# Moving operands at other byte offsets, and eight loads and three fills issued by GpSimd, in a one-core decoder layer

## The chip, the core and the metric

The kernel runs on one core of a Trainium2 chip. The metric is the device time of one launch in microseconds, the median of several runs. The engines have short names here: PE is TensorE (its matmuls), PEld its loads of the stationary operand, DVE is VectorE, ACT is ScalarE, POOL is GpSimd, and SP is the engine whose queue issues most transfers. Each engine takes its instructions in the order in which they were built.

## What is computed

One layer of a decoder, for 256 tokens of width 2048, in float32. It has three parts, each followed by a layer norm over `ALPHA * h + f(h)`:

```python
mix = hybrid_mixer(h, w_in, w_out, ...)     # S5 state space | stick-breaking heads | NSA heads, then w_out
xa = memory_cross_attention(h, mem, wq, wkv, wo)
ff = conv_ffn(h, w_up, conv_w, conv_b, w_down)   # 2048 -> 11264, conv, gated gelu, 5632 -> 2048
```

In the NSA attention the logits of every head get a bias that depends on the distance of query and key, `rel_bias[t5_bucket(dist)]`. The kernel holds that bias in the tile `slab`, with 16 heads of 256 columns each for every partition.

## The kernel before

**Products in three passes.** Every weight is read from memory as float32 in chunks of 128 x 1024 (`raw`, four buffers, issued by SP). ACT copies a chunk rounded into `hi`, DVE subtracts and writes the rest into `lo` (lines 291 and 292, three buffers of each). Activations are stored in two such parts as well. A product is then three matmuls: hi with hi, hi with the activations' rest, lo with hi. PE needs two operands for each: a stationary one of 128 columns, which a weight load brings in, and a moving one that streams through.

**Which operand moves.** Where the result is wanted as features by tokens (`mm3`, lines 306 to 308: all input projections but the values, the up-projection), the weights are stationary and 256 columns of activations move. Where it is wanted as tokens by columns (`mm3x`, lines 314 to 316: value projections, `w_out`, `wo`, `w_down`), the activations are stationary and `hi` and `lo` move, 512, 304 or 256 columns at a time. The residual's 2048 columns are done as three blocks of 512 and two of 256 (`RES_COLS`). One 128-row slice of the inner dimension gives six such matmuls a column block, three for each half of the tokens. So `w_out` (16 slices) has 288 matmuls of 512 columns and 192 of 256. `w_down` has 44 slices, the first 16 of which are in the tile `A` and the others in the tile `act`: 288 of 512 columns with `A` and 504 with `act`. Its last 256 columns are done last, and four of their chunks are held in the tiles `mix0` to `mix3`, which move in place of `hi` and `lo` there.

**Where the tiles lie.** Each pool follows the one before it in SBUF, and `gap` puts unused bytes between some. From the built program's addresses, counted modulo 256 bytes: all `hi` and `lo` buffers begin at 32, `A` and `mix0` to `mix3` at 224, `act` and `ox` (the cross-attention's output) at 32, `mixk` at 32. All slices of them that a matmul reads step by multiples of 512 bytes, but for those of 304 columns. So the distance from the stationary operand's start to the moving one's, modulo 256, is 192 in nearly all of `mm3`, 64 in `mm3x` where `A` or a `mix` tile is stationary, and 0 where `act` or `ox` is.

**The end of the mixer.** Four things stand here in a row on PE, and the same order is kept in both kernels: the keys (`nsa_keys`, 24 matmuls for each chunk of weights, results in three banks `pj`), the gate of the S5 group (`s5_out`, tile `s5zs`, four groups of 12 matmuls), the first three query projections (48 matmuls each), and then the NSA attention's first scores (lines 1011 and 1012, into `mx`), which need the queries' second part `nq` from DVE (line 971). Later queries and `w_out` run between the pieces of the attention. The gate goes gelu (line 765, ACT), table load, split into `s5zs`, matmuls, exp (line 782, ACT), reciprocal and product (lines 786 and 787, DVE), split into `mix0`.

`slab` shares its space with the tile `Es` of the S5 scan, so its eight loads of 256 KB (line 962) may start once the scan's last output matmuls have read `Es`. They were written for ACT's queue, and ACT issues them there before it goes on:

```python
        with self.lane("first"):
            for c in range(n):
                src = bass.AP(g_dr.tensor, g_dr.offset + 127 - c, ...)
                self.nc.scalar.dma_start(self.slab[c:128:n], src)
```

A scheduler orders each engine's instructions when the kernel is built, by priorities of lanes and its own model of times. It is run anew for a changed kernel.

Of the kernel before, what the change touches and what calls it, by code (L numbers as in the profile page):

```python
# [9 lines left out]
F32R = mybir.dt.float32r  # L10
# [15 lines left out]
BIG = 1e30  # L26
# [8 lines left out]
RES_COLS = ((0, 512), (512, 512), (1024, 512), (1536, 256), (1792, 256))  # L35
CST_AT = 3
SKEW = 16
NORM0, NORM1, HOLD = 3, (2,), 2
TABLE_PACE, SCAN_PACE = 0.8, 2.8
BUCKET_FROM = [16, 21, 27, 35, 46, 59, 77, 99, 128, 166, 216]  # L40
# [157 lines left out]
class Program:  # L198
# [24 lines left out]
        self.pq = pool("pq", 1, space=bass.MemoryType.PSUM)  # L223
        self.dram = pool("dram", 1, space=bass.MemoryType.DRAM)

    def gap(self, name, size):

        self.ctx.enter_context(self.tc.tile_pool(name=f"gap_{name}", bufs=1)).tile(
            [128, size // 4], F32, name=f"gap_{name}")

    @contextmanager
# [31 lines left out]
        return self.pq.tile([128, 512], F32, name="pb")  # L263


    def weights(self, src, n=1024, into=None):
        nc = self.nc
        with self.lane("split"):
            raw = self.wraw.tile([128, 1024], F32, name="raw")
            self.last_load = nc.sync.dma_start(raw[:, :n], src)  # L270
            parts = self.split_chunk(raw, n, into)
        self.mm_marks = self.mm_marks[1:] + [self.last_mm]
        self.credit += self.pace
        while self.credit >= 1:
            self.credit -= 1
            self.step()
        return parts
# [2 lines left out]

        return self.background is not None and next(self.background, None) is not None

    def split_chunk(self, raw, n, into=None):
        nc = self.nc
        with self.lane("split"):
            if into is not None:
                hi, lo = into
            else:
                hi = self.whi.tile([128, 1024], F32R, name="hi")
                lo = self.wlo.tile([128, 1024], F32R, name="lo")  # L290
            self.last_hi = nc.scalar.copy(hi[:, :n], raw[:, :n])  # L291
            self.last_lo = nc.vector.tensor_sub(lo[:, :n], raw[:, :n], hi[:, :n].bitcast(F32))  # L292
            hold = self.holds.pop(0) if self.holds else None
            if hold is not None:
                self.after(self.last_lo, hold)
        return hi, lo
# [38 lines left out]
    def to_cols(self, w, X, cols, kk, k0, k1):  # L335

        ps = [self.pj.tile([128, 512], F32, name="pj") for _ in range(2)]
        for c in range((k1 - k0) // kk):
            parts = self.weights(w[c], kk * cols)
            for tok in range(2):  # L340
                k = k0 + c * kk
                self.chunk_cols(ps[tok], parts, X, tok, cols, range(k, k + kk), k == k0,
                                k + kk == k1)
        return [p[:, :cols] for p in ps]
# [10 lines left out]
    def to_residual(self, w, X, k0, k1, scaled=True, final=True, load=None, late=0, keep=(),  # L355
                    between=None):

        first = 0  # L360
        if final:
            self.st = self.stat.tile([128, 2, len(RES_COLS), 6], F32, name="st")
        early = len(RES_COLS) - late
        for c0, n in RES_COLS[:early]:
            kk, cs = 1024 // n, slice(c0, c0 + n)
            if load is not None:
                with self.lane("split"):
                    self.after(self.nc.sync.dma_start(self.R[:, :, cs], load[:, :, cs]),
                               self.last_load)
            steps = (k1 - k0) // kk  # L370
            ps = self.to_cols(w[first:first + steps], X, n, kk, k0, k1)
            first += steps
            for tok in range(2):
                self.add(ps[tok], tok, c0, n, scaled, final)
        if not late:
            return
        chunks = []
        for g, (c0, n) in enumerate(RES_COLS[early:]):
            kk = 1024 // n
            for k in range(k0, k1, kk):  # L380
                chunks.append((g, c0, n, range(k, k + kk), w[first]))
                first += 1
        held, beside = {}, None
        turning = min(3, len(chunks) - len(keep))
        fixed = range(len(keep))
        order = list(range(len(chunks)))
        for tok in range(2):
            left = [(k1 - k0) * n // 1024 for _, n in RES_COLS[early:]]
            ps = {}
            for i in order:  # L390
                g, c0, n, ks, src = chunks[i]
                if i not in held:
                    held[i] = self.weights(src, into=keep[i] if i in fixed else None)
                new = g not in ps
                if new:
                    ps[g] = self.pj.tile([128, 512], F32, name="pj")
                left[g] -= 1
                self.chunk_cols(ps[g], held[i], X, tok, n, ks, new, left[g] == 0)
                if left[g] == 0:
                    self.add(ps[g][:, :n], tok, c0, n, scaled, final)  # L400
                    if beside is not None:
                        next(beside, None)
            if tok == 0:
                beside = between()
                next(beside, None)
                again = order[len(keep):-turning]
                for i in again:
                    del held[i]
                if again:
                    order = order[-turning:] + list(fixed) + again  # L410
# [540 lines left out]
    def nsa_slab(self):  # L951


        g_dr, n = self.g_dr, 128 // SKEW

        self.nq = self.nsp.tile([128, 8, 2, 256], F32R, name="nq")
        self.slab = self.slabp.tile([128, NH, 256], F32, name="slab", tag="Es")
        with self.lane("first"):
            for c in range(n):
                src = bass.AP(g_dr.tensor, g_dr.offset + 127 - c,  # L960
                              [[384 - n, SKEW], [SKEW * 384, NH], [1, 256]])
                self.nc.scalar.dma_start(self.slab[c:128:n], src)

    def nsa_queries(self):
        a, V, S, q = self.a, self.nc.vector, self.nc.scalar, self.nq
# [8 lines left out]
    def nsa(self):  # L974
        nc, a, V, S = self.nc, self.a, self.nc.vector, self.nc.scalar
# [10 lines left out]


        pc = p.tile([128, 2, NH, 32], F32, name="pc")
        V.memset(pc, 0.0)
        tcs = [p.tile([128, 2, 4, NC_], F32, name=f"tcs{i}") for i in range(2)]  # L990
        for t in tcs:
            V.memset(t[:, 0], BIG)
        halves = lambda t: t.rearrange("p (c k) -> p c k", c=2)
        for quad in range(4):
            o = self.pq.tile([128, 2, 256], F32, name="pa")
            start = [None, None]
            for b in range(2):
                n = 128 if b else 128 + NK
                for gl in range(2):
# [3 lines left out]
                    for r in range(2):  # L1003
                        h = h0 + r
                        kh, kl = (k[:, h // 8, gl].rearrange("p c n -> p (c n)") for k in ks[b])
                        t = qcol(h)
# [198 lines left out]
    def cross_attention(self, H):  # L1205
        nc, a, V, S = self.nc, self.a, self.nc.vector, self.nc.scalar
        mm = nc.tensor.matmul
        scale = 128.0 ** -0.5
        with ExitStack() as st:
            p = st.enter_context(self.tc.tile_pool(name="xap", bufs=1))  # L1210
            w = st.enter_context(self.tc.tile_pool(name="xaw", bufs=2))
            ox = p.tile([128, 4, 2, 256], F32R, name="ox")
# [59 lines left out]

    def ffn(self, H):
        nc, a, V, S = self.nc, self.a, self.nc.vector, self.nc.scalar
        self.gap("f", 128)
        p = self.ctx.enter_context(self.tc.tile_pool(name="ffp", bufs=1))
        w = self.ctx.enter_context(self.tc.tile_pool(name="ffw", bufs=2))
        cv = p.tile([128, NFF, 2, 4], F32, name="cv")
# [5 lines left out]
        for i in range(NFF):  # L1284
            c = []
# [50 lines left out]
```

## Time and profile before

| | us |
|---|---|
| median of 3 runs (1293.86 to 1295.22) | 1294.0 |
| the profiled execution's own time | 1293.79 |
| its span | 1292.0 |
| PE busy | 1254.6 (97%) |
| DVE busy | 883.8 (68%) |
| ACT busy | 659.9 (51%) |
| POOL busy | 13.3 (1%) |

A matmul's own duration in the profile holds the time that it takes to run through the array, and matmuls overlap. What one costs in a full stream is the distance from its start to the next one's. A stretch in which PE does one kind of work without a break therefore gives the pace: its length over the number of matmuls that the program has there.

### The profile page before, as it was taken

To read this page: it belongs to the slowest core of one execution; us is meant where nothing else is said; L and a number is where in the kernel's file an instruction comes from. 1 tells how busy PE (TensorE), PEld (TensorE's weight loads), DVE (VectorE), ACT (ScalarE), POOL (GpSimd) and SP (SyncE) were. 2 spreads that over 40 slices of the span, in tenths; PEclk is the share of its full clock that TensorE was granted. 3 is DMA by queue.
4 is the path that set the end of the run, shared out by engine and by line. 5 is a ranking of instruction groups with operands and counts; after the bars stand their busy time and mean duration, and the time that the engine had idled before them with its cause. 6 is when DMAs were issued, how large, how long until landed. Compare 5 with 4: busy or idle time off the path is not lost.

```text
span 1292.0 us, 23010 instructions
## 1 busy us (share of the span) xinstructions
PE 1254.6 (97%) x9222; PEld 1160.8 (90%) x9222; DVE 883.8 (68%) x1510; ACT 659.9 (51%) x1032; POOL 13.3 (1%) x23
## 2 busy tenths in 40 slices
PE   7999999999999999899999999999999999999996
PEld 7788898988779899799999999999999988888896
DVE  7799896877765675776666666666666654544557
ACT  6884434666554355455555555555555543334342
POOL 0200000000000000000000000000000000000000
PEclk9999999999999999999999999999999999999998
DMA  8653348633447564445555565565655755656573
GB/s 306 192 167 128 99 137 224 186 117 103 131 168 279 189 208 151 137 142 194 192 192 195 196 195 191 191 193 194 196 196 190 254 193 195 195 184 199 187 228 130
DMA packets 68886, 237.37 MB, mean 184 GB/s; under 512 B 7787, under 2 KB 10652, under 8 KB 68012
## 3 DMA queue, kind: packets, MB, share of 16 engines
q1 hardware_dynamic: 64720, 230.21, 53.7%
q10 hardware_dynamic: 3276, 3.47, 1.2%
q0 software_dynamic: 784, 2.23, 0.9%
q8 instruction: 72, 1.18, 0.4%
q14 instruction: 34, 0.28, 0.1%
HBM read 231.82 MB, written 2.49 MB: 181 GB/s over the span
## 4 chain that ended last, share of the span: by engine, by line
PE 76%; DVE 3%; ACT 1%; issue 1%; DMA 0%; DVEq 0%; ACTq 0%
PE pj L306 14%; PE pj L307 14%; PE pj L308 14%; PE pj L314 9%; PE pj L316 9%; PE pj L315 9%; PE pa L1048 2%; DVE lo L292 1%; PE mx L1011 1%; PE mx L1012 1%; DVE R L1144 1%; DVE R L1149 1%; PE op L1041 0%; PE pb L1041 0%; ACT hi L291 0%
## 5 line engine op out<-in xcount | busy, mean ns | idle before, releaser
L292 DVE TENSOR_TENSOR lo<-raw,hi 128x1024 fp32r<-128x1024 f32 (+2 forms) x403 | 488.5, 1212 | 339.0 <-ACT hi L291 337.9
L291 ACT CAST hi<-raw 128x1024 fp32r<-128x1024 f32 (+2 forms) x403 | 419.8, 1042 | 510.7 <-PE pj L307 276.4
L307 PE MATMUL pj<-mix,hi 128*128 128x256 f32 x1380 | 381.9, 277 | 0.0
L306 PE MATMUL pj<-mix,hi 128*128 128x256 f32 x1380 | 381.1, 277 | 0.0
L308 PE MATMUL pj<-mix,lo 128*128 128x256 f32 x1380 | 381.0, 276 | 0.0
L307 PEld LDWEIGHTS pj<-mix,hi 128*128 128x128 f32 x1380 | 259.2, 188 | 0.1
L308 PEld LDWEIGHTS pj<-mix,lo 128*128 128x128 f32 x1380 | 259.2, 188 | 0.1
L306 PEld LDWEIGHTS pj<-mix,hi 128*128 128x128 f32 x1380 | 259.1, 188 | 0.2
L306 PE MATMUL pj<-A,hi 128*128 128x256 f32 x496 | 141.2, 288 | 8.6 <-ACT hi L291 8.6
L308 PE MATMUL pj<-A,lo 128*128 128x256 f32 x496 | 139.2, 288 | 4.2 <-DVE lo L292 4.0
L307 PE MATMUL pj<-A,hi 128*128 128x256 f32 x496 | 140.4, 286 | 0.0
L306 PEld LDWEIGHTS pj<-A,hi 128*128 128x128 f32 x496 | 95.9, 194 | 11.2 <-ACT hi L291 9.3
L308 PEld LDWEIGHTS pj<-A,lo 128*128 128x128 f32 x496 | 94.6, 194 | 8.1 <-DVE lo L292 5.6
L307 PEld LDWEIGHTS pj<-A,hi 128*128 128x128 f32 x496 | 96.1, 194 | 1.9 <-issue 1.9
L315 PE MATMUL pj<-lo,act 128*128 128x512 f32 (+1 forms) x280 | 96.8, 347 | 0.0
L316 PE MATMUL pj<-hi,act 128*128 128x512 f32 (+1 forms) x280 | 96.8, 347 | 0.0
L315 PE MATMUL pj<-lo,A 128*128 128x512 f32 (+2 forms) x288 | 96.3, 336 | 0.0
L316 PE MATMUL pj<-hi,A 128*128 128x512 f32 (+2 forms) x288 | 95.6, 333 | 0.0
L314 PE MATMUL pj<-hi,A 128*128 128x512 f32 (+2 forms) x288 | 91.0, 334 | 0.0
L314 PE MATMUL pj<-hi,act 128*128 128x512 f32 (+1 forms) x280 | 89.7, 347 | 0.0
L315 PEld LDWEIGHTS pj<-lo,A 128*128 128x128 f32 x288 | 54.1, 188 | 6.5 <-issue 1.1
L315 PEld LDWEIGHTS pj<-lo,act 128*128 128x128 f32 x280 | 52.9, 189 | 6.6
(324 smaller groups left out, 1809.5 us busy)
## 6 DMA issues: line engine op xcount, KB each, us to landing
raw<-in_w_up SPq DMA_DIRECT2D x176, 512.0 KB, 4.2
raw<-in_w_down SPq DMA_DIRECT2D x92, 512.0 KB, 3.3
raw<-in_win_c SPq DMA_DIRECT2D x48, 512.0 KB, 3.9
raw<-in_w_out SPq DMA_DIRECT2D x32, 512.0 KB, 4.0
raw<-in_win_sv SPq DMA_DIRECT2D x8, 512.0 KB, 4.7
raw<-in_wk_m SPq DMA_DIRECT2D x8, 512.0 KB, 4.9
raw<-in_wv_m SPq DMA_DIRECT2D x8, 512.0 KB, 4.2
raw<-in_wq SPq DMA_DIRECT2D x8, 512.0 KB, 4.1
```

What stands on the lines that cost most here:

```text
L291: self.last_hi = nc.scalar.copy(hi[:, :n], raw[:, :n])
L292: self.last_lo = nc.vector.tensor_sub(lo[:, :n], raw[:, :n], hi[:, :n].bitcast(F32))
L306: mm(ps, hi, ah, start=start, stop=False)
L307: mm(ps, hi, al, start=False, stop=False)
L308: self.last_mm = mm(ps, lo, ah, start=False, stop=stop)
L314: mm(ps, ah, hi, start=start, stop=False)
L315: mm(ps, ah, lo, start=False, stop=False)
L316: self.last_mm = mm(ps, al, hi, start=False, stop=stop)
L1011: mm(zs, q[:, t, gl, qs], kh[:, 0:m], start=True, stop=False)
L1012: mm(zs, q[:, t, gl, qs], kl[:, 0:m], start=False, stop=True)
L1048: ins = mm(o[64 * r:64 * r + 64, gl, 128 * c:256], vv[:, c, v, :], pt[:, k0:k1], start=start[r] is None, stop=False, skip_group_check=True)
L1144: ins = V.scalar_tensor_tensor(r, r, mean, self.gb[:, 0, c0:c1], ALU.subtract, ALU.mult)
```

## The change

`hi` and `lo` buffers become 1088 columns wide in place of 1024, so each takes 4352 bytes, 17 times 256. Chunks for `mm3x` are written from column 48 on (192 bytes) where the column block is 512 wide, and from column 32 on (128 bytes) where it is 256. Those for 304 columns, for `mm3`, and the held chunks stay at column 0. A gap of 192 bytes ahead of the cross-attention's pool moves `ox`, and the gap ahead of the feed-forward's pool goes from 128 to 64 bytes, which moves `act`. In the built program `A`, `act`, `ox` and `mix0` to `mix3` now all begin at 224 modulo 256, `mixk` stays at 32, and the matmuls' distances change so:

| moving columns | stationary | matmuls | start of moving, stationary, distance before | after |
|---|---|---|---|---|
| 256 | `A`, `mix0` to `mix3` | 576 | 32, 224, 64 | 160, 224, 192 |
| 256 | `act`, `ox` | 384 | 32, 32, 0 | 160, 224, 192 |
| 512 | `A`, `mix0` to `mix3` | 672 | 32, 224, 64 | 224, 224, 0 |
| 512 | `act`, `ox` | 528 | 32, 32, 0 | 224, 224, 0 |
| 512 (held in `A`) | `ox` | 48 | 224, 32, 192 | 224, 224, 0 |

The loads of `slab` are issued by POOL, and three fills (`pc` and two `tcs`, tiles of the attention) go from DVE to POOL.

```diff
+MOVING_AT = {512: 48, 256: 32}
...
-                hi = self.whi.tile([128, 1024], F32R, name="hi")
-                lo = self.wlo.tile([128, 1024], F32R, name="lo")
+                hi = self.whi.tile([128, 1088], F32R, name="hi")
+                lo = self.wlo.tile([128, 1088], F32R, name="lo")
+                at = MOVING_AT.get(cols, 0)
+                hi, lo = hi[:, at:], lo[:, at:]
...
-            parts = self.weights(w[c], kk * cols)
+            parts = self.weights(w[c], kk * cols, cols=cols)
...
-                    held[i] = self.weights(src, into=keep[i] if i in fixed else None)
+                    held[i] = self.weights(src, into=keep[i] if i in fixed else None, cols=n)
...
-                self.nc.scalar.dma_start(self.slab[c:128:n], src)
+                self.nc.gpsimd.dma_start(self.slab[c:128:n], src)
...
-        V.memset(pc, 0.0)
+        nc.gpsimd.memset(pc, 0.0)
...
-            V.memset(t[:, 0], BIG)
+            nc.gpsimd.memset(t[:, 0], BIG)
...
+            self.gap("x", 192, st)
...
-        self.gap("f", 128)
+        self.gap("f", 64)
```

ACT's queue at the end of the S5 scan, before. `kh0` and `kh1` are parts of the keys, `s5u` is the scan's output, `hi_2616` and `hi_2646` are the weights of the last key projection and `hi_2682` those of the gate:

```order
L938 CAST kh0_2091<-pj_2401 64x2x128 x2
L962 DMA slab_2794<-g_dr_1514 16x16x256 x8
L291 CAST hi_2616<-raw_2614 128x1024
L291 CAST hi_2646<-raw_2644 128x1024
L938 CAST kh0_2091<-pj_2468 64x2x128 x2
L765 ACTIVATE s5u_198<-s5u_198 128x1024
L253 ACT_TABLE_LOAD
```

And now:

```order
L943 CAST kh0_2091<-pj_2401 64x2x128 x2
L770 ACTIVATE s5u_198<-s5u_198 128x1024
L254 ACT_TABLE_LOAD
L984 ACTIVATE gate_2116<-gate_2116 128x96
L296 CAST hi_2616<-raw_2614 128x1024
L943 CAST kh0_2091<-pj_2468 64x2x128 x2
L304 CAST s5zs_2538<-s5u_198 128x4x256
L296 CAST hi_2646<-raw_2644 128x1024
```

The eight loads are gone from this queue, and the gelu with its table load now stands ahead of the two splits.

DVE's queue at the first scores of the attention, before (`pj_2803` and `pj_2868` are the first two query projections, `mx_3334` the first scores):

```order
L292 TENSOR_TENSOR lo_3002<-raw_2999,hi_3001 128x1024
L989 MEMSET pc_3326 128x1024
L992 MEMSET tcs0_3328 128x60
L992 MEMSET tcs1_3329 128x60
L300 TENSOR_TENSOR mix0_2535<-s5z_2768,mix0_2535 128x256
L971 SCALAR_TENSOR_TENSOR nq_2793<-pj_2803,nq_2793 64x256
L971 SCALAR_TENSOR_TENSOR nq_2793<-pj_2868,nq_2793 64x256
L292 TENSOR_TENSOR lo_3032<-raw_3029,hi_3031 128x1024
L1015 ISA tt_3339,mn_3340<-mx_3334,slab_2794 128x128
```

And now:

```order
L297 TENSOR_TENSOR lo_3002<-raw_2999,hi_3001 128x1024
L305 TENSOR_TENSOR mix0_2535<-s5z_2768,mix0_2535 128x256
L976 SCALAR_TENSOR_TENSOR nq_2793<-pj_2803,nq_2793 64x256
L976 SCALAR_TENSOR_TENSOR nq_2793<-pj_2868,nq_2793 64x256
L297 TENSOR_TENSOR lo_3032<-raw_3029,hi_3031 128x1024
L976 SCALAR_TENSOR_TENSOR nq_2793<-pj_2803,nq_2793 64x256
L976 SCALAR_TENSOR_TENSOR nq_2793<-pj_2868,nq_2793 64x256
L1020 ISA tt_3339,mn_3340<-mx_3334,slab_2794 128x128
```

The fills have left, and the second pair of `nq` parts, which stood between two heads' softmax steps, now stands ahead of the first.

On POOL, whose last work before was the fill of `kl1`, the program now ends:

```order
L936 MEMSET kl1_2544 128x1024
L967 DMA slab_2794<-g_dr_1514 16x16x256 x8
L994 MEMSET pc_3326 128x1024
L997 MEMSET tcs0_3328 128x60
L997 MEMSET tcs1_3329 128x60
```

Nothing of POOL's stands behind these. PE's order is the same up to the first scores; within the attention the pieces of later queries and of `w_out` fall elsewhere among its steps, and from the memory's keys on it is the same again.

## Rows read from the trace of the kernel before

**Rows 1.** The chain that ended last, by engine (the page, part 4).

```profile
PE 76%; DVE 3%; ACT 1%; issue 1%; DMA 0%; DVEq 0%; ACTq 0%
```

**Rows 2.** Windows: stretch, length, busy of PE, PEld, DVE, ACT, POOL; clock; DMA.

```profile
390.94:412.71 21.77, 21.77 (x194) 21.77 (x193) 11.77 (x14) 8.45 (x8) 0.00 (x0) 1.00 0.87 313
1037.65:1059.63 21.98, 21.98 (x99) 18.04 (x97) 11.35 (x12) 10.77 (x12) 0.00 (x0) 1.00 0.58 192
1059.63:1097.73 38.10, 38.10 (x170) 31.54 (x168) 17.37 (x15) 14.70 (x14) 0.00 (x0) 1.00 0.58 193
1217.84:1229.14 11.30, 11.30 (x97) 11.30 (x96) 6.98 (x8) 4.20 (x4) 0.00 (x0) 1.00 0.55 173
1229.14:1249.29 20.15, 20.15 (x170) 20.15 (x169) 10.78 (x9) 9.56 (x10) 0.00 (x0) 1.00 0.67 211
1250.71:1255.03 4.32, 4.32 (x39) 4.32 (x38) 3.68 (x6) 2.10 (x2) 0.00 (x0) 1.00 0.88 262
535.82:541.43 5.61, 5.61 (x26) 4.50 (x25) 4.70 (x14) 0.41 (x2) 0.00 (x0) 1.00 0.01 3
```

**Rows 3.** ACT in order of time around the loads of `slab` (start, us; idle before, releaser).

```profile
214.40 9.10 ACTq L962 DMA_DIRECT2D slab<-g_dr  x8
223.59 1.99 ACT L291 CAST hi<-raw 128x1024 fp32r<-128x1024 f32 x2 [9.04 <-DMA slab<-g_dr]
226.38 1.06 ACT L765 ACTIVATE s5u<-s5u 128x1024 f32<-128x1024 f32 x1
227.45 1.28 ACT L253 ACT_TABLE_LOAD   x1
```

**Rows 4.** PE in order of time, from the keys to the first scores.

```profile
222.17 0.28 PE L308 MATMUL pj<-A,lo 128*128 128x256 f32 x1
224.69 0.39 PE L306 MATMUL pj<-A,hi 128*128 128x256 f32 x1 [2.24 <-ACT hi L291]
225.95 0.47 PE L308 MATMUL pj<-A,lo 128*128 128x256 f32 x1 [0.76 <-DVE lo L292]
...
237.24 0.39 PE L306 MATMUL pj<-s5zs,hi 128*128 128x256 f32 x1 [2.01 <-ACT s5z L782]
...
258.25 0.28 PE L308 MATMUL pj<-A,lo 128*128 128x256 f32 x1
...
262.48 0.36 PE L1011 MATMUL mx<-kh,nq 128*128 128x256 f32 x1 [2.98 <-DVE nq L971]
```

**Rows 5.** Windows of two stretches with a lower clock, columns as in rows 2.

```profile
226.10:229.50 3.40, 3.40 (x17) 3.40 (x18) 1.75 (x4) 3.35 (x5) 0.00 (x0) 0.50 1.12 206
263.60:267.10 3.50, 3.50 (x19) 3.50 (x18) 2.37 (x13) 0.99 (x4) 0.00 (x0) 0.51 0.16 67
```

**Rows 6.** DVE in order of time, from the stalled split to the first bias.

```profile
214.96 0.47 DVE L190 SCALAR_TENSOR_TENSOR s5u<-s5u,s5prm,pa 128x256 f32<-128x256 f32 x1
224.67 1.23 DVE L292 TENSOR_TENSOR lo<-raw,hi 128x1024 fp32r<-128x1024 f32 x1 [8.78 <-ACT hi L291]
...
237.55 1.76 DVE L786 RECIPROCAL s5z<-s5z 128x128 f32<-128x128 f32 x2
...
256.03 0.91 DVE L989 MEMSET pc<- 128x1024 f32 x1 [0.16 <-DVE lo L292]
256.90 0.18 DVE L992 MEMSET tcs<- 128x60 f32 x2
...
259.31 0.29 DVE L1015 CUSTOM_DVE_ANT_0 tt<-mx,slab 128x128 f32<-128x128 f32 x1
```

**Rows 7.** Transfers: issuing queue, count, KB each, median us from issue to landing.

```profile
slab<-g_dr ACTq DMA_DIRECT2D x8, 256.0 KB, 10.3
s5us<-Ec POOLq DMA_DIRECT2D x12, 128.0 KB, 5.3
```

**Rows 8.** POOL in order of time, its transfers of `s5us`.

```profile
35.40 5.04 POOL L496 DMA_DIRECT2D s5us<-Ec  x9 [31.98 <-ACT Ec L299]
41.31 1.76 POOL L496 DMA_DIRECT2D s5us<-Ec  x3 [0.87 <-DMA s5us<-Ec]
```

More of the change, by code (lines that the diff above doesn't have):

```diff
@@ L224, in __init__, with gap @@
         self.dram = pool("dram", 1, space=bass.MemoryType.DRAM)
-    def gap(self, name, size):
-        self.ctx.enter_context(self.tc.tile_pool(name=f"gap_{name}", bufs=1)).tile(
+    def gap(self, name, size, ctx=None):
+        (ctx or self.ctx).enter_context(self.tc.tile_pool(name=f"gap_{name}", bufs=1)).tile(
             [128, size // 4], F32, name=f"gap_{name}")
@@ L263, in turn, with weights @@
         return self.pq.tile([128, 512], F32, name="pb")
-    def weights(self, src, n=1024, into=None):
+    def weights(self, src, n=1024, into=None, cols=None):
         nc = self.nc
@@ L270, in weights @@
             self.last_load = nc.sync.dma_start(raw[:, :n], src)
-            parts = self.split_chunk(raw, n, into)
+            parts = self.split_chunk(raw, n, into, cols)
         self.mm_marks = self.mm_marks[1:] + [self.last_mm]
@@ L281, in step, with split_chunk @@
         return self.background is not None and next(self.background, None) is not None
-    def split_chunk(self, raw, n, into=None):
+    def split_chunk(self, raw, n, into=None, cols=None):
         nc = self.nc
```

## The prediction, made before the changed kernel was run

> **What bounds the kernel now.** I read the chain of waits first: PE has 76% of it and no other engine more than 3% [rows 1]. So time is won where a matmul gets cheaper or where PE stands still, and the change touches both. For the first I read windows in which PE does one kind of work without a break. For the second I read PE in order of time around the loads of `slab`, then ACT and DVE there, which PE waits for.
>
> **Pace and offset.** The reader is to divide a window's length by the matmuls that the program has in it (the count in the row also holds the few that only reach in over an edge). With 256 moving columns [rows 2]: distance 192 (row 1, the keys of the memory, 192 matmuls) 21.77 / 192 = 113.4 ns; distance 64 (row 4, `A` stationary, 96) 11.30 / 96 = 117.7 ns; distance 0 (row 5, `act` stationary, 168) 20.15 / 168 = 119.9 ns; distance 0 with both at 224 (row 6, held chunks with `A`, 36) 4.32 / 36 = 120.0 ns. With 512 columns: distance 64 (row 2, `A`, 96) 21.98 / 96 = 229.0 ns; distance 0 (row 3, `act`, 168) 38.10 / 168 = 226.8 ns; distance 192 (row 7, chunks held in `A` with `ox`, 24) 5.61 / 24 = 233.8 ns. Rows 2 to 5 lie behind one another in `w_down`, at full clock, with the same transfers and with DVE and ACT half idle, so what differs is the address. The two rows at distance 0 with 256 columns agree though one has its operands at 32 and the other at 224: that speaks for the distance and against the place. I therefore take the distance as what sets the pace: 192 is best for 256 columns, 0 is best for 512.
>
> The change puts every stream of 256 columns at distance 192 and every one of 512 at 0. Worked out by the counts of the table in the section on the change, all on PE's own stream, where nothing hides it:
> - 576 matmuls from 117.7 to 113.4: 576 x 4.3 = 2.5 us.
> - 384 from 119.9 to 113.4: 384 x 6.5 = 2.5 us.
> - 672 from 229.0 to 226.8: 672 x 2.2 = 1.5 us.
> - 48 from 233.8 to 226.8: 0.3 us; 528 stay at 226.8.
>
> Sum 6.8 us. No row shows moving operands at 160, nor 512 columns with both at 224. The bounds are therefore the best and the worst pace of that width in any row. For 256 columns the worst is 120.0, 576 x 2.3 = 1.3 us lost. For 512 it is 233.8, 672 x 4.8 + 528 x 7.0 = 6.9 us lost. So the term lies between -6.8 and +8.2 us. I take -6.8, since the distance explains all seven rows. `hi` and `lo` as stationary operands keep their 32 modulo 256, so the up-projection, at distance 192 already, costs what it did. The wider buffers and the offsets cost ACT and DVE nothing: they write as many columns. The gaps move only tiles that ACT and DVE use beside PE.
>
> The Trainium skill (SBUF — State Buffer, section "Who interferes with whom") gives PE two independent read ports, one for the moving operand and one for the weight load, and says that PE never waits on anyone. By that rule no offset could change a pace, and this term would be 0. The seven windows disagree with it, with 113.4 against 120.0 ns.
>
> **The loads of `slab` leave ACT.** Issuing eight loads keeps ACT from 214.40 to 223.5; the two splits behind them had been ready, as their 9.04 us of wait for nothing but these transfers say [rows 3]. DVE sits 8.78 us behind ACT [rows 6]. PE still has split weights until 222.17, then waits 2.24 us for `hi` and 0.76 us for `lo` [rows 4], and after these waits the granted clock falls to half for 3.40 us [rows 5], which costs half of that, 1.7 us. These three, 4.7 us, hang on ACT's queue directly and go with it: that is the lower bound.
>
> What ACT did late made more late: gelu and table load at 226.38 and 227.45 [rows 3], in the new order next after the scan's output at 215.43 [rows 6]. From there come PE's 2.01 us in the gate and the 2.98 us at the first scores, which wait for `nq` behind DVE's backlog [rows 4], and the second fall of the clock, again half of 3.50 us [rows 5]. These are 2.0 + 3.0 + 1.7 = 6.7 us more, so the upper bound is 11.4 us.
>
> To choose, I walk the new orders with the rows' durations. ACT: gelu 215.4 to 216.5, table load to 217.8, gate to 218.1, `hi_2616` to 219.1, with `lo` at 220.3; PE wants them at 222.3, no wait. `hi_2646` waits for its buffer until 219.5, comes behind two other pieces of ACT at 221.9, `lo` at 223.2; wanted at 225.0. The gate's weights are split at 224.9 and `s5zs` at 222.0; wanted at 227.8. The gate's second group finds its bank free. The third and fourth need the exp of the first and second, at 230.0 and 232.2, wanted at 230.7 and 232.1. The first query projection needs the last of the keys' parts out of its bank: behind a reciprocal pair of 1.76 us [rows 6] and a split that is 234.3, wanted at 233.7, so 0.6 us of waiting is left. Three projections of 48 at 113.4 ns bring PE to 250.7 in place of 258.4 [rows 4]. The last splits for them come at 246.4 (wanted at 248.0), the first `nq` at 249.6 (wanted 250.7), their second pair at 251.6, before PE, which now has 24 matmuls of the fourth projection ahead of them, asks for it at about 254.5. So the walk gives nearly all of the 11.4 us. But it is a chain of some twenty steps on ACT and DVE with slacks of 1 to 1.6 us at its end, and the attention behind it is interleaved anew, with 118 changes between projection and attention matmuls on PE against 108. I take 9.0 us.
>
> The loads on POOL: nothing is queued behind them but the fills, so POOL may wait. DVE first reads `slab` at 259.31 [rows 6], by the walk at about 252. POOL issues nine transfers in 5.04 us, 0.56 us each, then waits 0.87 us for one to land [rows 8], and its own take 5.3 us to land against 10.3 us for these on ACT's queue [rows 7]. Eight at 0.6 us and 10.3 us for the last end at about 230, more than 20 us early; the cost is nothing as long as that cover holds. The weights that now load at the same time are wanted every 2.7 us and have four buffers; the gate's 48 matmuls need no new ones. The fills took DVE 0.91 + 0.18 us [rows 6] inside its backlog; the walk holds that gain. POOL can start them only when the S5 tiles beneath are free, as DVE did, and the first reader of `tcs` stands behind two steps of softmax. So they are put at 0, with 1 us lost as the bound if DVE has to wait for POOL.
>
> The Trainium skill (SBUF — State Buffer, section "SBUF: two separate sides") warns of transfers issued from the GpSimd queue: their descriptors cannot be written while DVE holds a port that the two share, and it advises the ACT or SP queue. By it these loads could land late and the fills could block. The issue of nine in 5.04 us shows no such wait.
>
> **The sum.** It is made against the profiled execution's own 1293.8 us, which is the median less 0.2. 1293.8 - 6.8 - 9.0 = 1278.0 us.
>
> **The rivals.**
> - Offsets do nothing, the differences being of the stage and not of the distance: 1293.8 - 9.0 = 1284.8 us. For it: each stage has its own tiles, so distance and tile go together. Against it: the equal pace of `act` at 32 and `A` at 224. It is also what the port rule named above would give. Chance 0.09.
> - Only the direct stall goes, and the gate's chain on DVE (reciprocals of 1.76 us a group, splits of 1.23 us [rows 6]) makes PE wait at the first scores as before: 1293.8 - 6.8 - 4.7 = 1282.3 us. For it: these steps stay in series on DVE. Against it: the 8.78 us in which DVE idled ahead of them are freed. Chance 0.21.
> - The distance rule fails for 512 columns with both at 224, and they run at 233.8: -1.5 becomes +6.9, 1278.0 + 8.4 = 1286.4 us. For it: the only moving operand at 224 with 512 columns has that pace, in the last window of [rows 2]. Against it: that one is at distance 192. Chance 0.09.
> - Slower: POOL lands the loads one at a time. At 10.3 us each the last is there at 214.4 + 82.4 = 296.8, 45 us after the walk's first reader, and PE, which takes its instructions in order, stands behind the scores' banks: about 1278 + 42 = 1320 us. It turns into a loss once a load takes more than (252 + 16 - 214.4) / 8 = 6.7 us; POOL's own 5.3 us one at a time would give 256.8 and only some 5 us of waiting. Against it: nine were in flight at once [rows 8]. Chance 0.04.
> - As forecast: 0.57.
>
> **How the numbers follow.** The likeliest is 1278.0. The low end is the upper bound of both terms and the rest of PE's small waits, 1293.8 - 6.8 - 11.4 - 2 = 1273.6, taken as 1273. The high end reaches to the third rival, 1287. Outside are the fourth rival, the forecast's own tails and the corners of two bad bounds at once, together under 0.2. Within 0.2% (2.6 us, about what a measurement of this kernel tells from no change) lies only a mix of rivals, offsets at their worst and 4.7 us won, chance 0.02. Faster 0.94, slower 0.04.
>
> **What would show it.** In the profile after: windows of `w_down` at about 113.4 ns (256 columns) and 226.8 ns (512) with `A` as with `act`; if they stay at 118 to 120 and 229, the first term is wrong, and if 512 columns rise to 234, the third rival is right. On ACT no wait of 9 us, on PE no idle time at the last key projection and no half clock after it; a half clock at the first scores would mean the second rival. On DVE the first bias step must not wait for a transfer of `slab`; if it does, it is the fourth. The up-projection must keep its pace.

## The result and the profile after

The changed kernel takes 1282.8 us (median of 4 runs, 1281.05 to 1284.53), against 1293.9 us for the kernel before on the same chip. The ratio is 0.9912, 95% interval [0.9895, 0.9929]. By the ratio that is 11.4 us less, between 9.2 and 13.6 us. Forecast were 15.8 us and 1278.0. The profiled execution took 1284.53 us, with a span of 1282.4 us (before: 1292.0).

**The paces.** These are windows of the changed kernel, with the columns of [rows 2]; in order they are 96 matmuls of 512 columns with `A`, 168 with `act`, then of 256 columns 96 with `A`, 168 with `act`, 120 with `act`, and 24 of 512 columns held in `A` with `ox`:

```profile
1030.08:1051.86 21.78, 21.78 (x98) 18.02 (x97) 11.36 (x12) 10.75 (x12) 0.00 (x0) 1.00 0.58 193
1051.86:1089.94 38.08, 38.08 (x169) 31.53 (x168) 17.39 (x15) 14.66 (x14) 0.00 (x0) 1.00 0.58 193
1209.62:1220.93 11.31, 11.31 (x98) 11.31 (x96) 6.98 (x8) 4.19 (x4) 0.00 (x0) 1.00 0.58 185
1220.93:1240.71 19.78, 19.78 (x170) 19.78 (x169) 10.85 (x9) 9.42 (x10) 0.00 (x0) 1.00 0.67 224
1246.47:1260.09 13.62, 13.62 (x123) 13.62 (x122) 7.98 (x10) 6.41 (x7) 0.00 (x0) 1.00 0.65 228
527.29:532.73 5.44, 5.44 (x27) 4.51 (x25) 4.66 (x14) 0.41 (x2) 0.00 (x0) 1.00 0.02 4
```

512 columns run at 226.9, 226.7 and 226.7 ns, as forecast. 256 columns run at 117.8 ns with `A`, which is the pace of before, at 117.7 ns with `act` and then, with the same tiles at the same addresses, at 113.5 ns. Between the two `act` windows lie 48 matmuls of held chunks at distance 0.

**ACT** after the scan's last output (compare [rows 3]), and **POOL** with the transfers:

```profile
216.56 1.06 ACT L770 ACTIVATE s5u<-s5u 128x1024 f32<-128x1024 f32 x1 [0.91 <-DVE s5u L191]
217.63 1.28 ACT L254 ACT_TABLE_LOAD   x1
219.12 1.04 ACT L296 CAST hi<-raw 128x1024 fp32r<-128x1024 f32 x1
...
232.45 1.04 ACT L296 CAST hi<-raw 128x1024 fp32r<-128x1024 f32 x1 [4.29 <-DMA raw<-in_win_c]
...
235.83 1.05 ACT L296 CAST hi<-raw 128x1024 fp32r<-128x1024 f32 x1 [1.08 <-DMA raw<-in_win_c]
```

```profile
215.75 4.49 POOL L967 DMA_DIRECT2D slab<-g_dr  x8 [31.62 <-DMA raw<-in_win_c]
251.89 0.96 POOL L994 MEMSET pc<- 128x1024 f32 x1 [31.65 <-DVE s5z L792]
```

The wait of 9.04 us is gone; gelu, table load and first split come in the new order, about 1 us after the walk's times. A new wait stands at 232.45: ACT, free from 228.2, waits for the first weights of the query projections. The transfer of the second weights stands in the chain of waits (start, us, what) and ends at 235.7. PE in order of time shows what hangs on ACT there, and DVE the first bias:

```profile
224.42 11.31 DMA raw<-in_win_c
```

```profile
234.81 0.38 PE L311 MATMUL pj<-s5zs,hi 128*128 128x256 f32 x1 [2.74 <-ACT s5z L787]
237.31 0.39 PE L311 MATMUL pj<-s5zs,hi 128*128 128x256 f32 x1 [0.80 <-ACT s5z L787]
256.11 0.28 PE L1016 MATMUL mx<-kh,nq 128*128 128x256 f32 x1
```

```profile
256.80 0.29 DVE L1020 CUSTOM_DVE_ANT_0 tt<-mx,slab 128x128 f32<-128x128 f32 x1 [0.32 <-PE mx L1017]
```

The exp of the gate stands behind the late split in ACT's queue, so PE waits 2.74 and 0.80 us for it. It reaches the first scores at 256.1; the walk said 250.7, before had 258.4. There the wait of 2.98 us [rows 4] and the half clock behind it [rows 5] are gone, and the first bias waits for PE and not for `slab`.

**The DMA engines** while `slab` is loaded (windows; the last three columns are PE's granted clock, the DMA engines' busy share and GB/s), and the transfers from 205 to 240 us, with the median us to landing:

```profile
220.00:224.00 4.00, 4.00 (x37) 4.00 (x36) 3.79 (x5) 3.90 (x8) 0.24 (x1) 1.00 1.04 204
228.00:232.00 4.00, 4.00 (x35) 3.87 (x33) 1.06 (x2) 0.15 (x1) 0.00 (x0) 1.00 1.03 257
```

```profile
slab<-g_dr POOLq DMA_DIRECT2D x8, 256.0 KB, 10.7
raw<-in_w_glu SPq DMA_DIRECT2D x2, 512.0 KB, 6.8
```

From 220 us on they are busy without a gap. `slab` takes as long as on ACT's queue [rows 7]; the weights issued meanwhile take 6.8 us (`in_w_glu`, the gate's) and 11 us (the first two of the query projections), where in the kernel before 4.1 and 4.3 us were usual.

### The profile page after: what moved, and what is told of

Its sections match the earlier page's. It is cut to its first block, busy times and chain, and to the rows that moved or that the text cites. A ratio compares the mean times of both kernels' runs of the same rounds, so it can differ in the third digit from the quotient of the medians.

```text
span 1282.4 us, 23034 instructions
## 1 busy us (share of the span) xinstructions
PE 1250.7 (98%) x9222; PEld 1157.6 (90%) x9222; DVE 882.1 (69%) x1507; ACT 659.7 (51%) x1032; POOL 18.9 (1%) x34
## 4 chain that ended last, share of the span: by engine, by line
PE 89%; DMA 4%; DVE 3%; ACT 3%; issue 1%; POOL 0%; SPq 0%; ACTq 0%; DVEq 0%
PE pj L311 17%; PE pj L313 17%; PE pj L312 17%; PE pj L319 10%; PE pj L320 10%; PE pj L321 10%; DMA raw<-in_win_u 2%; PE pa L1053 2%; DMA s5us<-Ec 1%; DMA raw<-in_win_c 1%; ACT hi L296 1%; PE pa L191 1%; DVE lo L297 1%; PE mx L882 1%; PE mx L1016 1%
## 5 line engine op out<-in xcount | busy, mean ns | idle before, releaser
L311 PEld LDWEIGHTS pj<-A,hi 128*128 128x128 f32 x496 | 94.7, 192 | 9.5 <-ACT hi L296 7.5
L312 PEld LDWEIGHTS pj<-A,hi 128*128 128x128 f32 x496 | 94.6, 192 | 1.6 <-issue 1.6
L321 PEld LDWEIGHTS pj<-hi,A 128*128 128x128 f32 x288 | 54.2, 188 | 5.0
```

Of the source, the lines that this page charges most:

```text
L311: mm(ps, hi, ah, start=start, stop=False)
L312: mm(ps, hi, al, start=False, stop=False)
L321: self.last_mm = mm(ps, al, hi, start=False, stop=stop)
```

## The experiments

Gains are one less the ratio to the kernel before, times 1294 us, with the 95% interval. The plain differences of the medians are 3.8, 5.6 and 6.5 us for the offsets, the loads and the fills alone, 0.7 to 1.2 us more than by the ratio; one expectation below quotes these.

**The offsets alone** (the changed kernel, loads and fills as before):

```diff
-                self.nc.gpsimd.dma_start(self.slab[c:128:n], src)
+                self.nc.scalar.dma_start(self.slab[c:128:n], src)
-        nc.gpsimd.memset(pc, 0.0)
+        V.memset(pc, 0.0)
-            nc.gpsimd.memset(t[:, 0], BIG)
+            V.memset(t[:, 0], BIG)
```

> The changed kernel with the eight loads of slab back on ACT's queue and the three fills back on DVE: the offsets and gaps alone, against the kernel before. Distance alone sets the pace (the forecast): 6.8 us faster, 1287.1 us, every window of 256 moving columns at 113.4 ns. Two paces at distance 192, one kept from the entry of the stream: 512 columns all at 226.7 ns (1.8 us won), of 256 columns only what `act` and `ox` had at 120 ns falls to 117.8 ns and one stretch after the held chunks reaches 113.5 ns, so about 3 us faster, 1291 us. Offsets do nothing: 1294 us. ACT waits 9 us with the loads again, and half clock shows again near 226 and 264 us.

1290.5 us, ratio 0.9976 [0.9964, 0.9988]: 3.1 us gained (1.6 to 4.7). Distance alone would have given 6.8. Windows of this kernel, 96 matmuls with `A` and 168 with `act`:

```profile
1214.68:1225.99 11.31, 11.31 (x97) 11.30 (x96) 6.99 (x8) 4.20 (x4) 0.00 (x0) 1.00 0.57 179
1225.99:1245.78 19.79, 19.79 (x171) 19.79 (x169) 10.85 (x9) 9.24 (x9) 0.00 (x0) 1.00 0.68 213
```

Both run at 117.8 ns. So do the keys of the memory (192 matmuls), the very stretch from which the forecast took 113.4 ns, at distance 192 as before:

```profile
387.71:410.32 22.61, 22.61 (x195) 22.61 (x194) 11.68 (x13) 8.42 (x8) 0.00 (x0) 1.00 0.83 305
```

ACT waits 9.23 us for the loads again, and the clock is at half again from 225.55. One thing differs from before. PE waits just as long at the first scores, but the clock did not fall behind that wait: the window shows it at full over 6 us, where in the kernel before it fell about 1 us after the wait [rows 4, 5].

```profile
261.25 0.36 PE L1016 MATMUL mx<-kh,nq 128*128 128x256 f32 x1 [2.97 <-DVE nq L976]
```

```profile
261.25:267.25 6.00, 6.00 (x52) 6.00 (x53) 5.76 (x25) 3.45 (x12) 0.00 (x0) 1.00 0.24 83
```

The fall of the clock is therefore not a fixed price of that wait, as the forecast had it.

**`mixk` at another place** (the kernel before; every other tile stays where it is):

```diff
-        self.gap("k", 64)
         self.hkp = pool(self.ctx, "hkp", 1)
+        self.gap("k", 64)
```

> The kernel before with the 64 byte gap ahead of mixk moved behind it, so that mixk moves from 224 and not 32 (its distance to hi and lo goes from 0 to 192, as that of all other tiles that move in the up-projection); nothing else moves. Distance alone sets the pace: the 276 matmuls with mixk fall from about 118 to 113.4 ns, 1.3 us faster. Two paces at distance 192, and mixk's slice at distance 0 is what brings PE into the faster one: the up-projection's 4224 matmuls run at 117.8 ns in place of 113.4 ns, up to 18.6 us slower, about 1312 us.

1310.3 us, ratio 1.0127 [1.0113, 1.0140]: 16.4 us slower (14.6 to 18.1). Here is the same stretch of the up-projection, first of the kernel before, then of this one:

```profile
600.00:1000.00 400.00, 400.00 (x3518) 400.00 (x3518) 264.63 (x366) 210.27 (x293) 0.00 (x0) 1.00 0.59 193
```

```profile
600.00:1000.00 400.00, 400.00 (x3398) 400.00 (x3398) 255.33 (x353) 202.90 (x283) 0.00 (x0) 1.00 0.57 187
```

3518 matmuls fit into 400 us before (113.7 ns) and 3398 now (117.7 ns). Some 94% of them read the same tiles at the same addresses as before. All that is new is that no slice at distance 0 comes between them. Moving one slice in sixteen to distance 192 thus made the other fifteen slower. This settles that distance 192 has two paces, and that a slice at distance 0 between them holds this stream in the faster one.

It does not settle what decides elsewhere. The three query projections (144 matmuls at distance 192) come ahead of everything that this edit moves, and up to them PE, ACT and DVE do the same work in the same order as in the kernel before. They ran at 113.5 ns there and at 117.8 ns here; in the changed kernel it was 118.3 ns. In this order:

```profile
242.03:258.37 16.34, 16.34 (x147) 16.34 (x146) 15.13 (x26) 9.03 (x14) 0.00 (x0) 1.00 0.54 179
242.80:259.77 16.97, 16.97 (x146) 16.97 (x145) 15.52 (x26) 8.90 (x14) 0.00 (x0) 1.00 0.57 180
239.08:256.11 17.03, 17.03 (x144) 17.03 (x145) 16.10 (x26) 9.55 (x16) 1.12 (x3) 1.00 0.55 184
```

Over the twelve profiles of this study they took 113.4 to 114.0 ns in five and 117.8 to 118.6 ns in seven. What differs ahead of them is when and how long PE waits, and at which clock; no run varied that alone.

**The first chunk at distance 0** (the changed kernel):

```diff
-            parts = self.weights(w[c], kk * cols, cols=cols)
+            parts = self.weights(w[c], kk * cols, cols=512 if c == 0 and turn and cols == 256 else cols)
```

> The changed kernel, but the first chunk of each 256 column block of win_v, w_out, wo and w_down that follows a 512 column one is written at column 48 (distance 0), all later ones at column 32 (distance 192) as before. Two paces: in w_down the first 24 matmuls run at 120 ns and all behind them at 113.4 in place of 117.8 ns: 72 x 4.4 + 168 x 4.4 less 24 x 2.2, about 1.0 us faster there, as much again in w_out's block, 1.5 to 2 us faster than the changed kernel in all, about 1281 us. Distance alone: nothing behind the first chunk changes, 24 x 2.2 ns a block, 0.1 us slower than the changed kernel, and the windows stay at 117.8 ns.

1283.5 us (1282.4 to 1285.9), ratio 0.9922 [0.9909, 0.9935]: no gain over the changed kernel that the times can tell. The windows of `w_down` did what the two paces ask. Behind the stretch of the first chunk come 60 with `A` at 113.7 ns, 168 with `act` at 113.3 ns and 120 at 113.5 ns:

```profile
1214.76:1221.58 6.82, 6.82 (x63) 6.82 (x61) 3.67 (x3) 3.15 (x3) 0.00 (x0) 1.00 0.64 216
1221.58:1240.62 19.04, 19.04 (x171) 19.04 (x169) 9.85 (x9) 9.26 (x9) 0.00 (x0) 1.00 0.62 209
1246.36:1259.98 13.62, 13.62 (x123) 13.62 (x121) 9.00 (x12) 6.41 (x7) 0.00 (x0) 1.00 0.70 246
237.40:240.80 3.40, 2.93 (x14) 2.64 (x13) 3.34 (x7) 1.64 (x4) 0.00 (x0) 0.50 0.51 172
```

From `w_down`'s start (1030.98, in the changed kernel 1030.08) to the end of these windows (1259.98 and 1260.09) it is 1.0 us shorter, as expected. Of `w_out`, where as much was expected, 95 matmuls in one stretch ran at 115.1 in place of 117.8 ns, which is 0.3 us. In this execution the last row, a half clock in the gate that the changed kernel's profile does not have, took 1.7 us of it back.

**The loads of `slab` alone** (the kernel before):

```diff
-                self.nc.scalar.dma_start(self.slab[c:128:n], src)
+                self.nc.gpsimd.dma_start(self.slab[c:128:n], src)
```

> The kernel before with only the eight loads of slab issued by POOL; offsets, gaps and fills as before. If the loads carry what the changed kernel gained beside the offsets: about 8 us faster, 1286 us, ACT's wait of 9 us gone, and a new wait of some 4 us of ACT for raw near 232 us, because the weight chunk's transfer shares the DMA engines with slab. If instead the new wait comes from the offsets or the fills: no wait for raw there, and 10 to 11 us faster. If only the direct stall goes: 4.7 us faster, 1289 us. All windows of 256 and 512 columns keep their paces of before.

1288.8 us, ratio 0.9963 [0.9950, 0.9975]: 4.8 us gained (3.2 to 6.5), as in the last case, but not by its mechanism. The wait for raw is there without offsets and fills, so it is the loads' own. ACT first, then PE:

```profile
231.99 1.04 ACT L291 CAST hi<-raw 128x1024 fp32r<-128x1024 f32 x1 [4.73 <-DMA raw<-in_win_c]
```

```profile
234.35 0.39 PE L306 MATMUL pj<-s5zs,hi 128*128 128x256 f32 x1 [3.18 <-ACT s5z L782]
238.62 0.35 PE L306 MATMUL pj<-A,hi 128*128 128x256 f32 x1 [1.13 <-DVE kl L939]
```

The wait at the first scores is gone here too. In this profile PE reaches the first scores 2.7 us sooner than in the kernel before (255.66 against 258.36) and ends the memory's keys 6.7 us sooner (406.02 against 412.71). At the start of `w_down` 5.0 us are left (1032.66 against 1037.65), because ahead of the feed-forward the clock stood at half for 6.80 us, against 3.40 us in the kernel before (its window stands further below):

```profile
543.50:550.30 6.80, 6.40 (x29) 6.14 (x30) 6.66 (x11) 1.71 (x7) 0.00 (x0) 0.50 0.28 94
```

So the gate took back part of the gain and the clock there some 1.7 us; that the rest equals the direct stall (4.7 us) is chance.

**The fills alone** (the kernel before):

```diff
-        V.memset(pc, 0.0)
+        nc.gpsimd.memset(pc, 0.0)
-            V.memset(t[:, 0], BIG)
+            nc.gpsimd.memset(t[:, 0], BIG)
```

> The kernel before with only the three fills (pc and two tcs) issued by POOL. The forecast put them at 0: within 0.5 us of the kernel before. If the sum of the offsets alone (3.1 us) and the loads alone (4.8 us) misses the whole change's 11.4 us because of the fills: about 3 us faster, 1291 us. If DVE has to wait for POOL at the first scores: 1 us slower.

1289.2 us, ratio 0.9959 [0.9945, 0.9973]: 5.3 us gained (3.5 to 7.1), where the forecast had 0. DVE at the first scores in the kernel before (the first bias between these rows is in [rows 6], at 259.31), and then in this one:

```profile
257.39 0.75 DVE L971 SCALAR_TENSOR_TENSOR nq<-pj,nq 64x256 fp32r<-64x256 f32 x2
258.17 1.23 DVE L292 TENSOR_TENSOR lo<-raw,hi 128x1024 fp32r<-128x1024 f32 x1
...
261.90 0.43 DVE L971 SCALAR_TENSOR_TENSOR nq<-pj,nq 64x256 fp32r<-64x256 f32 x1
```

```profile
257.51 0.75 DVE L971 SCALAR_TENSOR_TENSOR nq<-pj,nq 64x256 fp32r<-64x256 f32 x2
258.29 1.23 DVE L292 TENSOR_TENSOR lo<-raw,hi 128x1024 fp32r<-128x1024 f32 x1
259.55 0.77 DVE L971 SCALAR_TENSOR_TENSOR nq<-pj,nq 64x256 fp32r<-64x256 f32 x2
260.34 0.29 DVE L1015 CUSTOM_DVE_ANT_0 tt<-mx,slab 128x128 f32<-128x128 f32 x1
```

The first pair of `nq` comes at the same time in both. The second pair stands behind two heads' biases before, and ahead of them here. So the order counts for more than the 1.1 us of the fills: without them the scheduler puts DVE's queue in another order, and the wait of 2.98 us and the half clock [rows 4, 5] go, while ACT's stall is still there. No run changed the order alone.

**The changed kernel with the fills back on DVE:**

```diff
-        nc.gpsimd.memset(pc, 0.0)
+        V.memset(pc, 0.0)
-            nc.gpsimd.memset(t[:, 0], BIG)
+            V.memset(t[:, 0], BIG)
```

> The changed kernel with the three fills back on DVE: offsets and loads of slab as changed. The fills alone gave 6.5 us, the loads alone 5.6 us and the offsets alone 3.8 us, together more than the whole change. If fills and loads each remove the same wait (PE's 3.0 us at the first scores, which nq's place in DVE's queue decides, with the half clock behind it): putting the fills back costs nearly nothing, 1283 to 1285 us, and PE has no wait at the first scores. If the fills carry a gain of their own: 4 to 6 us slower than the changed kernel, 1288 us.

1285.9 us (1285.0 to 1289.8), ratio 0.9938 [0.9926, 0.9950]: 8.0 us gained (6.5 to 9.6). That is 2 to 3 us short of the changed kernel, nearer to the first case than to the second. DVE and PE at the scores, and the memory's keys (192 matmuls but one, which in [rows 2] ran at 113.4 ns):

```profile
255.92 0.43 DVE L976 SCALAR_TENSOR_TENSOR nq<-pj,nq 64x256 fp32r<-64x256 f32 x1
```

```profile
256.50 0.36 PE L311 MATMUL pj<-A,hi 128*128 128x256 f32 x1 [0.22 <-DVE nq L976]
383.81:406.50 22.69, 22.69 (x194) 22.66 (x193) 11.68 (x12) 8.34 (x9) 0.00 (x0) 1.00 0.69 263
```

With the loads off ACT, one piece of the second pair stands ahead of the biases even with the fills, and PE waits 0.22 us. Fills and loads remove the same wait; whichever comes second finds most of it gone. The keys ran at 118.8 ns in this execution, against 114.4 ns in the changed kernel's, another 0.8 us.

**`slab` paced** (the changed kernel; two loads at once on POOL, the other six on SP, each behind a load of weights):

```diff
             self.last_load = nc.sync.dma_start(raw[:, :n], src)
+            if self.later:
+                self.after(nc.sync.dma_start(*self.later.pop(0)), self.last_load)
...
-                self.nc.gpsimd.dma_start(self.slab[c:128:n], src)
+                if c < 2:
+                    self.nc.gpsimd.dma_start(self.slab[c:128:n], src)
+                else:
+                    self.later.append((self.slab[c:128:n], src))
```

> The changed kernel, but only the first two loads of slab are issued by POOL at once; the other six are issued by SP, one behind each of the next six loads of weights. If slab's eight loads together fill the DMA engines (their share stood at 1.0 from 220 to 236 us) and that made the load of the first query weights take 11 us: the wait of 4.3 us of ACT for raw near 232 us goes, PE's idle time of 3.0, 1.1 and 0.4 us in the gate goes, and the time is up to 4.4 us below that of the changed kernel, about 1279 us. If the late weights come from something else (the place of the loads in SP's queue, the gate's own chain): the gate keeps its idle time, and the time stays at 1283 us. If SP's queue, now with 8 loads behind one another, is held up by slab: new waits for raw between 235 and 250 us, and slower than the changed kernel.

1280.6 us (1279.0 to 1281.7), ratio 0.9886 [0.9871, 0.9901]. On the same chip the changed kernel took 1283.8 (below). ACT, then the DMA engines, then PE:

```profile
228.60 1.05 ACT L298 CAST hi<-raw 128x1024 fp32r<-128x1024 f32 x1 [1.01 <-ACT kh L945]
```

```profile
228.00:232.00 4.00, 4.00 (x36) 4.00 (x35) 2.75 (x6) 2.77 (x5) 0.00 (x0) 1.00 1.04 276
```

```profile
235.24 0.35 PE L313 MATMUL pj<-A,hi 128*128 128x256 f32 x1 [0.58 <-DVE kl L946]
252.27 0.28 PE L1021 MATMUL mx<-kh,nq 128*128 128x256 f32 x1
```

The first query weights are split at 228.6 in place of 232.5, with no wait for raw. PE's waits of 2.74 and 0.80 us in the gate are gone, the longest left is 0.58 us, and PE is at the first scores at 252.3. The engines are still full from 228 on. So a full DMA share alone makes no wait here; what changed is which transfers stand in front, for the weights now go ahead of most of `slab`. The bytes are the same. The edit also moves six loads from POOL's queue to SP's, and no run paced them on POOL, so order and queue are not told apart.

**The changed kernel once more**, on the same chip as the run above and the next:

> The changed kernel once more, on the same chip as the paced loads and both together, so that differences of 1 to 4 us can be read between them: 1283 us.

1283.8 us (1282.5 to 1284.3), ratio 0.9911 [0.9895, 0.9928]. No run of the paced kernel is as slow as the fastest of these.

**Both, paced `slab` and the first chunk at distance 0** (the two diffs above together):

> The paced loads of slab of the run before and the first chunk of each 256 column block of win_v, w_out, wo and w_down at distance 0 together. If both reasons hold: some 4 us from the gate and 1.0 us in w_down (216 matmuls of 256 columns more at 113.4 ns) with some 0.5 us in w_out, about 1277 to 1279 us. If the DMA reason falls: about 1282 us, w_down's windows at 113.4 ns all the same.

1279.9 us (1279.3 to 1280.1), ratio 0.9881 [0.9868, 0.9895]: 15.4 us gained (13.6 to 17.1). The expectation was 1277 to 1279. `w_down` again has its paces of 113.3 ns, and against the changed kernel the runs lie wholly apart. Against the paced kernel the medians differ by 0.7 us, which the ranges do not tell apart. It is the fastest of all versions tried.

**More first chunks at distance 0** (the run above, and the first key and first query projection as well):

```diff
-                hi, lo = self.weights(w[t, half])
+                turn = half == 0 and w is self.a["win_c"] and t in (12, 16)
+                hi, lo = self.weights(w[t, half], cols=512 if turn else None)
```

> The run with both (paced slab, first chunks at distance 0), and in addition the first chunk of weights of the first NSA key projection and of the first query projection written at column 48, where the weights are stationary and the activations in A move: 24 matmuls each at distance 0 ahead of streams at distance 192. Two paces: the query projections behind it, which ran at 118.3 ns, run at 113.4 ns, 120 x 4.9 = 0.6 us, and part of the keys as much, about 1 us in all, 1279 us. If what is entered from plays no part where the weights are stationary, or the stream falls back at its pauses: the window of the three query projections stays at 118 ns and the time at 1280 us.

1280.7 us, ratio 0.9886 [0.9874, 0.9899]: no gain. The keys (115 matmuls) did run at 114.3 ns, but only behind a pause for the scan; the 120 query matmuls right behind the chunk ran at 117.8 ns:

```profile
215.90:229.04 13.14, 13.14 (x116) 13.14 (x116) 10.00 (x14) 10.76 (x17) 1.16 (x2) 1.00 0.79 220
238.74:252.88 14.14, 14.14 (x123) 14.14 (x121) 13.17 (x23) 8.30 (x14) 1.12 (x3) 1.00 0.83 238
```

The expectation failed. Coming from distance 0 is not enough by itself. In `w_down` and the up-projection, where it worked, the moving operand's start changed at the switch; here the stationary one's did. Whether that is the reason was not tried, and it cannot be all: the query projections run at either pace without such a chunk, too.

## Why the prediction came out as it did

The time lies inside the range and the sign is right, but the forecast was 4.8 us too low, and the terms went wrong in both directions. That the sum still came near is partly luck: a gain put at nothing, that of the fills, stands in for some of what the offsets and the gate fell short.

**512 columns: right.** 226.7 to 226.9 ns with `A` and with `act`, 226.7 in place of 233.8 for the held chunks. The 1.8 us are there, and the rival of 233.8 ns at 224/224 is out.

**256 columns: mis-sized, about 1.9 us in place of 5.0.** The step that failed is "I therefore take the distance as what sets the pace". The distance is part of it: `act` fell from 119.9 to 117.7 ns (168 x 2.2 = 0.4 us) and, behind the held chunks, to 113.5 (120 x 6.4 = 0.8 us, and 0.3 us in the last 48); some 0.4 us lie in the mixer's value projection, where a stretch of 50 matmuls with `A` fell from 117.8 to 113.8 ns. But distance 192 has two paces, 113.4 and 117.8 ns, and row 1 of [rows 2], from which 113.4 was taken, happened to be in the faster one: the same keys ran at 117.8 ns in the run of the offsets alone. All seven rows fit the rule because only one of them had 256 columns at distance 192. That `A` showed no gain in `w_down` (117.7 and 117.8 ns) is no proof that offsets do nothing: before, it was at distance 64, which runs at that pace too. With the first chunk at distance 0 the full 113.4 came.

By the Trainium skill (SBUF — State Buffer, section "Who interferes with whom"), under which PE's two reads are independent, `mixk` could not have cost anything by its place; it cost 16.4 us. The measurement decides.

**The loads off ACT: right in the steps, wrong in one cover.** The step that failed is "The weights that now load at the same time are wanted every 2.7 us and have four buffers; the gate's 48 matmuls need no new ones". The buffers that should have covered them were not full: the first query weights were issued at 221.4, into engines that stood at a share of 1.04. That the DMA share was 1.12 in [rows 5], with `slab` in flight, was a row that could have been read so. ACT was stalled by `slab` itself then, so nobody missed the weights. With the loads paced, PE reaches the first scores at 252.3. The walk said 250.7, with projections at 113.4 ns, as before, where they ran at 118.3 (144 x 4.9 = 0.7 us), and with 0.6 us of idle time behind the gate, where the paced run has 0.58. The walk thus held to about 1 us once the weights came in time.

**The fills: put at 0 for a wrong reason.** The step that failed is "So they are put at 0". They gave 5.3 us alone. They were costed as 1.1 us of DVE inside a backlog; what they change is the place of `nq` in DVE's queue. The order of the changed kernel showed the second pair ahead of the first bias, and the walk used it, but I did not ask which edit had put it there. Beside the loads little of it is left (2 to 3 us by the run with the fills back on DVE), since the loads remove the same wait. The sum of the parts, 3.1 + 4.8 + 5.3 = 13.2 us against 11.4 for the whole, points the same way, but by less than its intervals.

**The rivals.** The time is nearly that of "only the direct stall goes" (1282.3), but by another mechanism: PE does not wait at the first scores. The new loss lies in the gate, where no rival had put it. POOL issues the eight loads in 4.49 us and nothing lands one at a time. The loss of which the Trainium skill warns for GpSimd's transfers (SBUF — State Buffer, section "SBUF: two separate sides") does not show in these rows: `slab` landed in 10.7 us against 10.3 on ACT's queue, and the fill of `pc` ran in 0.96 us against 0.91 on DVE. No row shows whether DVE held the shared port at the time.

**What stays open.** What turns a stream at distance 192 into the faster pace when it does not come from distance 0, and why it failed in the last run. And one loss elsewhere: before the feed-forward the clock stood at half for 6.80 us in the changed kernel's profile, against 3.40 us before, some 1.7 us. It was 6.8 us in six of the twelve profiles and 3.4 us in the other six, and no run was made for it. The changed kernel first, then the kernel before:

```profile
540.60:547.40 6.80, 5.74 (x27) 5.42 (x27) 6.55 (x14) 2.31 (x7) 0.00 (x0) 0.50 0.23 77
```

```profile
550.40:553.80 3.40, 3.12 (x15) 2.92 (x15) 3.31 (x6) 1.33 (x5) 0.00 (x0) 0.50 0.00 0
```

## What to carry to other kernels

A pace that is read from windows belongs to the window's history as well as to its addresses: before a rule goes into a sum, look for the same tiles at the same addresses in two windows and in two runs, and move one tile alone to test it. When transfers leave a stalled engine, ask what else is in flight at that moment, since a stall hides the queue behind it; where the DMA share is 1, put what is wanted first in front. And where a scheduler orders the queues, an edit of 1 us can be worth 5 by what it puts elsewhere, and two edits that remove the same wait do not add up.

## What the runs showed of the hardware

- Matmuls of 256 columns at one distance (192) have two steady paces, 113.4 and 117.8 ns, at the same addresses; with the same order of work up to them, the query projections ran at either. One slice in sixteen at the slower distance 0 kept the up-projection in the faster one; taking it away cost 16.4 us.
- 512 columns had one pace for each distance in the long streams of all kernels: 226.7 to 226.9 ns at 0, 228.9 to 229.1 at 64, 233.6 to 233.8 at 192 (24 matmuls).
- Eight loads of 256 KB in a row held ACT for 9.10 us and POOL for 4.49 us; SP issued its six, one at a time, in 0.54 to 0.65 us each, the first as here:

```profile
221.30 0.65 SPq L273 DMA_DIRECT2D slab<-g_dr  x1
```

- The same wait of 3.0 us at the same place was followed by a half clock in the kernel before and by full clock in the run of the offsets alone.
